# Low parts of weight blocks moved to GpSimd in a two-layer hybrid backbone

## The chip, the core and the metric

The kernel runs on one core of a Trainium2 chip. The metric is the device time of one execution in microseconds (us), as the median of several runs. The core has TensorE (matrix products, PE in the profile; its weight loads are PEld), VectorE (DVE), ScalarE (ACT), GpSimd (POOL) and the SyncE queue (SP), which here issues the DMAs.

## The reference, cut to what matters

Two layers work on 256 latent tokens and 256 context tokens of width 1024, in float32. Each layer does:

```python
h = rmsnorm(x, g1) * (1 + sc1) + sh1            # sc, sh, g: 6 modulation vectors from c @ w_mod
rx, rg, cq, ckv, kr, dq, dk, dv, mg = split(h @ w_in)
# 1. recurrence: conv of width 4 on rx, gates r, i = sigmoid(block-diagonal products),
#    a = exp(-8 r softplus(-lam)), b = sqrt(1 - a^2) i x,  h_t = a_t h_(t-1) + b_t, both ways
# 2. latent attention, 16 heads: o_b
# 3. differential attention, 8 heads of two maps:
o_c = (softmax(s q1 k1^T) - lam * softmax(s q2 k2^T)) @ v
# merge: three gated projections, then one output projection
x = x + g1 * ((ga * ((y_a * gelu(rg)) @ w_br_a) + gb * (o_b @ w_br_b) + gc * (norm(o_c) @ w_br_c)) @ w_out)
x = x + g2 * ffn(rmsnorm(x, g2) * (1 + sc2) + sh2)   # SwiGLU, hidden width 2816
```

The second layer computes queries and outputs for the 256 latent tokens only; its keys, values and recurrence still cover all 512.

## The kernel before

**Weights in two parts.** Every large product is made from three products of reduced-precision (`fp32r`) operands: a float32 matrix is split into a high part (the value rounded to `fp32r`) and a low part (the value less the high part), and `mm3` (lines 199 to 202) adds high x high, high x low and low x high in PSUM. In the trace these are the TensorE lines L200, L201 and L202.

Weights come in blocks of 128 x 1024 float32 (512 KB). `wload` (lines 156 to 181) takes a staging tile `st`, issues its DMA on SP's queue, takes a pair `wh`, `wl`, and calls `split`. In `split` (lines 136 to 141) ScalarE writes the high part with an activation, and VectorE writes the low part with one subtraction; both carry L138 in the trace, and the same line also splits activations, from PSUM or SBUF. Staging tiles and pairs come from rings of `WB = 3`. In layer 1 the ring is longer by two of each, which live in other tiles: pairs in `room`, staging tiles in a part of `acc`. So a low part shows as `wl<-st,wh` or as `room<-acc,room`.

**Order.** A planner (the tile framework) puts all instructions of each engine in one list by priority; each engine then works through its own list in order and waits at its head by semaphores. Weight splits get a priority ahead of their place in the program, by `first_by[0]` (90, or 600 in the recurrence of layer 1). Generators that yield pieces of matmul work stand in `queue`; `fill(ns)` lets them issue about that many ns of work between steps of the attentions and the recurrence.

**The two parts of a layer that the change touches.** First the differential attention. For four pairs of heads, `diff_proj` makes queries, keys and values (`gemm_tm`, six blocks a pair); meanwhile W_BB's projection of the latent attention's result (`gemm_fm`, eight blocks) runs. For each head `diff_prep` transposes and splits queries and keys, `diff_sc` makes the scores of both maps for each block of 128 queries, finds the row maximum (L621), exponentiates (L623) and merges the two maps (L966: `p1 = p2 * factor + p1`), `probs_T` transposes, `diff_pv` multiplies with the values. Then the recurrence, for four pairs of channel blocks: `rnn_rx` (projection and convolution, L1034), `rnn_rec` (gates from a block of `wlru`, L1056 to L1069, then two scans a block, L1082 and L1086), `rnn_rg` (projection and gelu, L1014 to L1017, product with the scan, L1108), with branch gates and W_BC's projections from `queue` (L1118, L1126, L1127). By the code these parts load 70 blocks in layer 0 and 72 in layer 1; the whole trace has 305 low parts on `wl` and 75 on `room`. In layer 0's recurrence the modulation vectors of later stages are made beside it (`mod_vectors`): VectorE multiplies streamed weights by the condition (L310), each such operation ordered behind the last low part by `issue_after(..., low[0])`, an edge without a semaphore.

**GpSimd before.** It holds only the Newton steps of some reciprocal roots (`rsqrt`, L222 to L225), for the queries of the latent attention (`rq`) and of the differential attention (`drq`), on tiles of 128 x 8 or 128 x 16.

Of the kernel before, what the change touches and what calls it, by code (L numbers as in the profile page):

```python
# [13 lines left out]
AF = mybir.ActivationFunctionType  # L14
ALU = mybir.AluOpType
# [48 lines left out]
def tile_hybrid(ctx: ExitStack, tc: tile.TileContext, xt, cvec, cwide, prm, row, dlam, rope, wmod, wmod0, wmodt, wfm, wcq, wckv, wuq, wukv, wlru, wfo, out):  # L64
    nc = tc.nc
    V = nc.vector
    A = nc.scalar
    G = nc.gpsimd
# [31 lines left out]
    def three_banks(stage):  # L100

        if spare[0] is not None:
            spare[0].close()
        spare[0] = ctx.enter_context(ExitStack())
        banks[0] = spare[0].enter_context(tc.tile_pool(name=stage, bufs=1, space=PSUM, reuse_waits="tile"))
# [27 lines left out]
    def f(ap):  # L133
        return ap.bitcast(F32)

    def split(dH, dL, src, scale=None):
        if scale is None:
            return A.activation(dH, src, AF.Copy), V.tensor_tensor(out=dL, in0=src, in1=f(dH), op=ALU.subtract)  # L138
        else:
            A.activation(dH, src, AF.Copy, scale=scale)  # L140
            V.scalar_tensor_tensor(out=dL, in0=src, scalar=scale, in1=f(dH), op0=ALU.mult, op1=ALU.subtract)

    ready = deque()
    hold = []
    low = [None]
    first_by = [WEIGHTS_FIRST]
    ring = {"st": 0, "w": 0}
    more = {"st": [], "w": []}

    def stage():  # L150
        ring["st"] = (ring["st"] + 1) % (WB + len(more["st"]))
        if ring["st"] < WB:
            return wp.tile([P, 1024], F32, tag="st", name="st")
        return more["st"][ring["st"] - WB]

    def wload(src, n=1024, now=True):

        if now and ready:
            key, H, L = ready.popleft()
            assert key == str(src)  # L160
            return H, L
        st = stage()
        nc.sync.dma_start(st[:, :n], src)
        ring["w"] = (ring["w"] + 1) % (WB + len(more["w"]))
        if ring["w"] < WB:
            H = wp.tile([P, 1024], F32R, tag="wh", name="wh")
            L = wp.tile([P, 1024], F32R, tag="wl", name="wl")
        else:
            H, L = more["w"][ring["w"] - WB]
        tc.cur_priority -= first_by[0]  # L170
        parts = split(H[:, :n], L[:, :n], st[:, :n])
        for b, a in zip(parts, hold):
            issue_after(b, a)
        hold.clear()
        low[0] = parts[1]
        tc.cur_priority += first_by[0]
        pace[1] += pace[0]
        while pace[1] >= 1:
            pace[1] -= 1
            slow_step(1)  # L180
        return H, L

    def ahead(srcs):

        ready.extend([(str(src), *wload(src, n, False)) for src, n in srcs])
# [5 lines left out]
    def slow_step(n):  # L191
        while n > 0 and slow:
            try:
                next(slow[0])
                n -= 1
            except StopIteration:
                slow.popleft()
# [30 lines left out]
    def issue_after(b, a):  # L228

        tc.add_manual_dep(b.ins, a.ins.name, mybir.DependencyInfo(mybir.DependencyClass.NoSync, mybir.DependencyReason.DATA), reason="one table for all")  # L230
# [6 lines left out]
    def fill(ns):  # L237

        credit[0] += ns
        while credit[0] > 0 and queue:  # L240
            try:
                credit[0] -= next(queue[0])
            except StopIteration:
                queue.popleft()
        if not queue:
            credit[0] = 0.0

    def flush():
        while queue:
            fill(1e6)  # L250
# [141 lines left out]
    def gemm_fm(l, widx, npair, xH, xL, TQ, ps_, consume, k_first=False):  # L392

        one = 2 * TQ <= 512
        for p in range(npair):
            if one:
                ps = ps_("ps0").rearrange("p (j n) -> p j n", j=2)
                pss = [ps[:, j, :] for j in range(2)]
            else:
                pss = [ps_(f"ps{j}")[:, :TQ] for j in range(2)]  # L400
            for hf in range(2):
                H, L = wload(*fm_block(l, widx, 2 * p + hf))
                H = H.rearrange("p (k n) -> p k n", n=256)
                L = L.rearrange("p (k n) -> p k n", n=256)
                order = [(j, kk) for kk in range(4) for j in range(2)] if k_first and p == 0 else [(j, kk) for j in range(2) for kk in range(4)]
                for i, (j, kk) in enumerate(order):
                    k = hf * 4 + kk
                    mm3(pss[j], H[:, kk, j * P:(j + 1) * P], L[:, kk, j * P:(j + 1) * P], xH[:, k, :TQ], xL[:, k, :TQ],
                        k == 0 and not (one and j == 1), k == KT - 1 and not (one and j == 0), one)
                    if k == KT - 1:  # L410
                        if not one:
                            consume(2 * p + j, 1, pss[j].unsqueeze(1))
                        elif j == 1:
                            consume(2 * p, 2, ps)
                    if i % 4 == 3 or k_first and p == 0 and i % 2 == 1:
                        yield (6 if k_first and p == 0 else 12) * mm_ns(TQ)

    def gemm_two(l, widx, xHL, consume):

        pss = [ps_any(f"ps{j}") for j in range(2)]  # L420
        for hf in range(2):
            H, L = wload(*fm_block(l, widx, hf))
            H = H.rearrange("p (k n) -> p k n", n=256)
            L = L.rearrange("p (k n) -> p k n", n=256)
            for j in range(2):
                for kk in range(4):
                    k = hf * 4 + kk
                    nc.tensor.matmul(pss[j], H[:, kk, j * P:(j + 1) * P], xHL(k), start=(k == 0), stop=False, skip_group_check=True)  # L428
                    nc.tensor.matmul(pss[j][:, :SEQ], L[:, kk, j * P:(j + 1) * P], xHL(k)[:, :SEQ], start=False, stop=(k == KT - 1), skip_group_check=True)  # L429
                if hf == 1:  # L430
                    consume(j, pss[j])
# [111 lines left out]
    for l in range(LAYERS):  # L543
# [7 lines left out]
        with ExitStack() as c1:  # L551
# [13 lines left out]
            def t_cq(name, dt=F32R):  # L565
                return tmp("cq", 10, dt=dt, name=name)
# [109 lines left out]
            def low_rank(wsrc, n, nf, toks, gcol, pss, extra, res, by_half=False):  # L676
# [26 lines left out]
                for i in range(nf):  # L703
                    pt = ps_tr("lrt")
                    for tt in toks:
                        nc.tensor.transpose(pt[:, tt * P:(tt + 1) * P], us[tt][:, i * P:(i + 1) * P], ident)
                    rH, rL = t_cq("rH"), t_cq("rL")
                    split(rH[:, :nt * P], rL[:, :nt * P], pt[:, :nt * P], scale=pm[:, gcol + i:gcol + i + 1])
                    res.append((rH, rL))
                    yield 4 * 109  # L710
# [70 lines left out]
            def mla_prep(h):  # L781
                qs, ks = mq[h // 4][0], mk[h // 2]
                ptq = ps_tr("trq")
                for tt in qtoks:
                    nc.tensor.transpose(ptq[:96, tt * P:(tt + 1) * P], qs[tt].rearrange("p (h d) -> p h d", d=96)[:, h % 4, :], ident)
                qH, qL = t_qk("qH"), t_qk("qL")
                split(qH[:96, :TQ], qL[:96, :TQ], ptq[:96, :TQ])
                ptk = ps_tr("trk")
                for tt in range(4):
                    nc.tensor.transpose(ptk[:96, tt * P:(tt + 1) * P], ks[tt][:, h % 2, :], ident)  # L790
                kH, kL = t_qk("kH"), t_qk("kL")
                split(kH[:96, :], kL[:96, :], ptk[:96, :], scale=gkk[:96])
                mqk[h] = (qH, qL, kH, kL)
# [328 lines left out]
            def branch_proj(widx, mgi, p, after=None):  # L1122
# [7 lines left out]

                yield from gemm_fm(l, widx + p, 1, oH, oL, TQ, ps_r[0], proj)

            three_banks(f"pair{l}")
            singles[0] = 1
            queue.append(diff_proj(0))
# [34 lines left out]
            for p in range(4):  # L1170
# [9 lines left out]
                for ns in rnn_rg(p):  # L1180
                    fill(ns * RG_SHARE[l])
            flush()
            for t in range(KT):
                y = t_cq("y", F32)
                nc.sync.dma_start(y[:, :TQ], yspill[:, t, :TQ])
                split(oH[:, t, :TQ], oL[:, t, :TQ], y[:, :TQ], scale=0.5)
# [309 lines left out]
```

## Time and profile before

| | |
|---|---|
| median of 3 runs | 1972.54 us (1972.23 to 1977.07) |
| the profiled execution's own time | 1974.12 us |
| its span, first to last instruction | 1972.3 us |
| busy: TensorE, VectorE, ScalarE, GpSimd | 1930.2, 1568.3, 1069.9, 58.8 us |
| TensorE's mean granted clock | 0.997 |

The profile is of one execution. Busy times are shares of its span; the ends of matmuls are modelled. "Idle before, releaser" is the time an engine stood idle just before a group of instructions, and what ended most of it.

### The profile page before, as it was taken

The page shows a single profiled execution, that of the slowest core. Times are in us where ns is not written, and L with a number is a line of the kernel's source. Part 1 is how long each engine was busy: PE and PEld are TensorE (multiplying, and loading weights), DVE is VectorE, ACT ScalarE, POOL GpSimd, SP SyncE. Part 2 cuts the span into 40 slices and gives each one's busy share as a digit, 9 for nine tenths or more (in the row PEclk, how much of TensorE's full clock was granted, in tenths as well). Part 3 has the DMA queues.
Part 4 walks back from the last instruction along what each step waited for, and adds up shares of the span by engine and source line. Part 5 has one row for each costly group of instructions (what it writes and reads, how often), then busy time and mean ns, then how long its engine had stood idle before and what let it go on. Part 6 is the DMA issues. An engine that isn't in the chain of part 4 may idle for free. (4 is left out here: it accounts for less than half of the span.)

```text
span 1972.3 us, 31832 instructions
## 1 busy us (share of the span) xinstructions
PE 1930.2 (98%) x11746; PEld 1666.3 (84%) x11746; DVE 1568.3 (80%) x3838; ACT 1069.9 (54%) x1975; POOL 58.8 (3%) x198
## 2 busy tenths in 40 slices
PE   7999999999999999999999999999999999899999
PEld 4888888988678878888888888988999788898888
DVE  5679965788798888789888876898688889966763
ACT  4568833455576663353233224798444678845552
POOL 0001000000000000000000000012010000000000
PEclk9999999999999999999999999999999999999999
DMA  8311122212234456536656653422322234474553
GB/s 291 99 41 51 53 65 77 76 55 67 70 102 129 140 191 197 184 127 201 196 191 201 200 176 115 151 64 76 128 93 80 65 123 143 156 231 150 185 189 108
DMA packets 91068, 258.16 MB, mean 131 GB/s; under 512 B 10144, under 2 KB 17312, under 8 KB 90656
## 3 DMA queue, kind: packets, MB, share of 16 engines
q1 hardware_dynamic: 90912, 256.13, 39.8%
q8 instruction: 92, 1.51, 0.3%
q14 instruction: 64, 0.52, 0.1%
HBM read 250.85 MB, written 5.24 MB: 130 GB/s over the span
## 5 line engine op out<-in xcount | busy, mean ns | idle before, releaser
L138 ACT ACTIVATE wh<-st 128x1024 fp32r<-128x1024 f32 (+4 forms) x305 | 308.4, 1012 | 367.8 <-PE ps L201 173.1
L138 DVE TENSOR_TENSOR wl<-st,wh 128x1024 fp32r<-128x1024 f32 (+4 forms) x305 | 354.2, 1162 | 125.5 <-ACT wh L138 122.0
L200 PE MATMUL ps<-hH,wh 128*128 128x512 f32 (+1 forms) x504 | 182.0, 361 | 3.8 <-ACT gt L1118 2.9
L202 PE MATMUL ps<-hH,wl 128*128 128x512 f32 (+1 forms) x504 | 180.6, 359 | 1.7 <-DVE wl L138 1.7
L201 PE MATMUL ps<-hL,wh 128*128 128x512 f32 (+1 forms) x504 | 181.3, 360 | 0.0
L200 PE MATMUL pst<-wh,hH 128*128 128x256 f32 x568 | 164.3, 289 | 0.0
L201 PE MATMUL pst<-wl,hH 128*128 128x256 f32 x568 | 162.1, 285 | 0.0
L202 PE MATMUL pst<-wh,hL 128*128 128x256 f32 x568 | 161.9, 285 | 0.0
L200 PE MATMUL ps<-h2H,wh 128*128 128x512 f32 (+1 forms) x368 | 139.1, 381 | 0.7 <-ACT h2H L379 0.7
L201 PE MATMUL ps<-h2L,wh 128*128 128x512 f32 (+1 forms) x368 | 139.5, 380 | 0.0
L202 PE MATMUL ps<-h2H,wl 128*128 128x512 f32 (+1 forms) x368 | 139.5, 380 | 0.0
L621 DVE TENSOR_REDUCE st<-S 128x1 f32<-128x512 f32 (+1 forms) x192 | 113.0, 596 | 21.4 <-ACT dp L623 11.2
L138 DVE TENSOR_TENSOR room<-acc,room 128x1024 fp32r<-128x1024 f32 (+3 forms) x75 | 87.6, 1169 | 30.6 <-ACT room L138 29.1
L200 PEld LDWEIGHTS pst<-wh,hH 128*128 128x128 f32 x568 | 108.6, 191 | 3.8 <-issue 3.3
L200 PEld LDWEIGHTS ps<-hH,wh 128*128 128x128 f32 x504 | 95.3, 189 | 19.3 <-ACT gt L1118 3.9
L202 PEld LDWEIGHTS pst<-wh,hL 128*128 128x128 f32 x568 | 108.5, 191 | 1.7 <-issue 1.4
L201 PEld LDWEIGHTS pst<-wl,hH 128*128 128x128 f32 x568 | 108.6, 191 | 1.1 <-issue 0.7
L202 PEld LDWEIGHTS ps<-hH,wl 128*128 128x128 f32 x504 | 95.2, 189 | 15.6 <-DVE wl L138 2.3
L310 DVE SCALAR_TENSOR_TENSOR ms<-ms,cb 128x512 f32<-128x512 f32 x160 | 107.3, 688 | 1.3
L138 ACT ACTIVATE room<-acc 128x1024 fp32r<-128x1024 f32 (+3 forms) x75 | 76.2, 1017 | 57.6 <-PE ps L201 20.5
L201 PEld LDWEIGHTS ps<-hL,wh 128*128 128x128 f32 x504 | 95.3, 189 | 12.8
L310 DVE SCALAR_TENSOR_TENSOR sq<-ms,cb 128x512 f32<-128x512 f32 x112 | 75.7, 689 | 31.9 <-DMA ms<-wmodt 31.0
(585 smaller groups left out, 5558.3 us busy)
## 6 DMA issues: line engine op xcount, KB each, us to landing
st<-wfm SPq DMA_DIRECT2D x224, 512.0 KB, 3.5
ms<-wmodt SPq DMA_DIRECT2D x160, 256.0 KB, 2.8
acc<-wfm SPq DMA_DIRECT2D x56, 512.0 KB, 3.5
st<-wfo SPq DMA_DIRECT2D x35, 512.0 KB, 3.5
mstage<-wmod SPq DMA_DIRECT2D x16, 512.0 KB, 5.3
acc<-wfo SPq DMA_DIRECT2D x9, 512.0 KB, 3.5
st<-wlru SPq DMA_DIRECT2D x7, 512.0 KB, 3.4
st<-wukv SPq DMA_DIRECT2D x13, 256.0 KB, 2.6
```

The lines of the kernel that those rows point to most:

```text
L138: return A.activation(dH, src, AF.Copy), V.tensor_tensor(out=dL, in0=src, in1=f(dH), op=ALU.subtract)
L200: nc.tensor.matmul(ps, wH, xH, start=start, stop=False, skip_group_check=skip)
L201: nc.tensor.matmul(ps, wH, xL, start=False, stop=False, skip_group_check=skip)
L202: nc.tensor.matmul(ps, wL, xH, start=False, stop=stop, skip_group_check=skip)
L310: issue_after(V.scalar_tensor_tensor(out=o, in0=st, scalar=1.0, in1=cb[:, v, :], op0=ALU.mult, op1=ALU.mult, accum_out=sums[:, i - i0, h, ...
L621: V.tensor_reduce(out=st[:, 0:1], in_=S, axis=AX.X, op=ALU.max, negate=True)
```

## The change

`split` gets an argument `by`, the engine that does the subtraction for the low part. `wload` passes `low_by[0]`, which is VectorE at first, GpSimd from the beginning of the differential attention of each layer to the end of its recurrence, and VectorE again after that. Splits of activations, which don't come through `wload`, stay on VectorE.

```diff
-    def split(dH, dL, src, scale=None):
+    def split(dH, dL, src, scale=None, by=V):
         if scale is None:
-            return A.activation(dH, src, AF.Copy), V.tensor_tensor(out=dL, in0=src, in1=f(dH), op=ALU.subtract)
+            return A.activation(dH, src, AF.Copy), by.tensor_tensor(out=dL, in0=src, in1=f(dH), op=ALU.subtract)
...
+    low_by = [V]
...
-        parts = split(H[:, :n], L[:, :n], st[:, :n])
+        parts = split(H[:, :n], L[:, :n], st[:, :n], by=low_by[0])
...
+            low_by[0] = G
             three_banks(f"pair{l}")
             singles[0] = 1
             queue.append(diff_proj(0))
...
             flush()
+            low_by[0] = V
             for t in range(KT):
                 y = t_cq("y", F32)
```

## Rows read from the trace of the kernel before

**Rows 1.** Summary of the page: busy time, share, instructions by engine.

```profile
PE 1930.2 (98%) x11746; PEld 1666.3 (84%) x11746; DVE 1568.3 (80%) x3838; ACT 1069.9 (54%) x1975; POOL 58.8 (3%) x198
```

**Rows 2.** Stretches: length, busy time of each engine, granted clock, DMA, GB/s.

```profile
262.00:545.00 283.00, 277.84 (x1885) 239.04 (x1880) 211.08 (x593) 136.04 (x311) 13.31 (x48) 1.00 0.22 71
545.00:727.00 182.00, 178.01 (x790) 144.50 (x789) 162.26 (x272) 132.30 (x198) 0.00 (x0) 1.00 0.43 137
1376.00:1590.00 214.00, 210.91 (x1603) 191.27 (x1602) 172.26 (x483) 106.73 (x221) 13.67 (x46) 1.00 0.28 89
1590.00:1720.00 130.00, 122.82 (x823) 112.89 (x822) 125.17 (x172) 110.14 (x153) 0.00 (x0) 0.99 0.43 140
```

**Rows 3.** TensorE's waits, 1590 to 1720: total us, times, longest us.

```profile
PE ps L202 <- DVE room L138: 5.5, 2, 4.1
```

**Rows 4.** VectorE's waits, 262 to 545.

```profile
DVE wl L138 <- ACT wh L138: 24.3, 14, 5.4
```

**Rows 5.** Groups of VectorE, 262 to 545: busy us, mean ns, idle before.

```profile
L138 DVE TENSOR_TENSOR wl<-st,wh 128x1024 fp32r<-128x1024 f32 x35 | 42.8, 1222 | 24.8 <-ACT wh L138 24.3
...
L966 DVE SCALAR_TENSOR_TENSOR dp<-dp,st,dp 128x512 f32<-128x512 f32 (+1 forms) x32 | 19.7, 615 | 0.7
```

**Rows 6.** Groups of VectorE by shape, 545 to 727.

```profile
L138 DVE TENSOR_TENSOR wl<-st,wh 128x1024 fp32r<-128x1024 f32 x33 | 40.2, 1218 | 7.9 <-ACT wh L138 7.8
...
L1017 DVE SCALAR_TENSOR_TENSOR ge<-ge,ps 128x512 f32<-128x512 f32 x8 | 5.5, 683 | 0.7 <-ACT ge L1016 0.7
L1126 DVE SCALAR_TENSOR_TENSOR gt<-gt,ps 128x512 f32<-128x512 f32 x8 | 5.4, 680 | 0.3 <-PE ps L202 0.2
...
L1015 DVE SCALAR_TENSOR_TENSOR ge<-ge,ps 128x512 f32<-128x512 f32 x8 | 5.4, 677 | 0.0
```

**Rows 7.** Groups of VectorE by shape, 1590 to 1720.

```profile
L138 DVE TENSOR_TENSOR wl<-st,wh 128x1024 fp32r<-128x1024 f32 x19 | 23.1, 1217 | 0.3 <-ACT wh L138 0.3
L138 DVE TENSOR_TENSOR room<-acc,room 128x1024 fp32r<-128x1024 f32 x13 | 15.9, 1220 | 0.8 <-ACT room L138 0.5 <-PE pg L201 0.3
...
L1126 DVE SCALAR_TENSOR_TENSOR gt<-gt,ps 128x512 f32<-128x512 f32 x4 | 2.7, 682 | 0.7 <-PE ps L202 0.7
L1015 DVE SCALAR_TENSOR_TENSOR ge<-ge,ps 128x512 f32<-128x512 f32 x4 | 2.7, 681 | 0.0
L1017 DVE SCALAR_TENSOR_TENSOR ge<-ge,ps 128x512 f32<-128x512 f32 x4 | 2.7, 676 | 0.0
```

**Rows 8.** GpSimd's lines in undisturbed stretches (264 to 269; 1420 to 1436.8): min/median/max ns.

```profile
L223 POOL TENSOR_TENSOR drqt<-drqt,drqv x3: 221/223/223, 265.2 to 267.6; 128x16 f32<-128x16 f32 x3
L223 POOL TENSOR_TENSOR drqt<-drqt,drqv x2: 202/202/202, 1435.2 to 1436.3; 128x8 f32<-128x8 f32 x2
L224 POOL TENSOR_SCALAR drqt<-drqt x3: 203/204/206, 265.5 to 267.9; 128x16 f32<-128x16 f32 x3
L224 POOL TENSOR_SCALAR drqt<-drqt x2: 197/198/198, 1435.5 to 1436.6; 128x8 f32<-128x8 f32 x2
```

**Rows 9.** Timeline of VectorE and GpSimd at three places: start us, length us.

```profile
459.06 1.22 DVE L138 TENSOR_TENSOR wl<-st,wh 128x1024 fp32r<-128x1024 f32 x1
459.26 1.09 POOL L223 TENSOR_TENSOR drqt<-drqt,drqv 128x16 f32<-128x16 f32 x1
...
1353.61 0.73 DVE L141 SCALAR_TENSOR_TENSOR kL<-trk,gkk,kH 96x512 fp32r<-96x512 f32 x1
1353.75 3.05 POOL L222 TENSOR_TENSOR rqt<-rq 128x8 f32<-128x8 f32 x1
1354.33 1.21 DVE L138 TENSOR_TENSOR wl<-st,wh 128x1024 fp32r<-128x1024 f32 x1
1355.54 1.21 DVE L138 TENSOR_TENSOR wl<-st,wh 128x1024 fp32r<-128x1024 f32 x1
...
221.07 0.68 DVE L138 TENSOR_TENSOR qL<-trq,qH 96x512 fp32r<-96x512 f32 x1
221.36 0.21 POOL L222 TENSOR_TENSOR rqt<-rq 128x16 f32<-128x16 f32 x1
```

## The prediction

> **What bounds the kernel now.** I read the summary first, then the stages, then the waits. TensorE's matmuls are busy in 1930.2 of 1972.3 us [rows 1], so whatever the edit takes off VectorE can at best give back TensorE's idle time. I cut the two parts of each layer that the edit touches by the first and last weight splits in the trace: 262 to 545 us (differential attention, layer 0), 545 to 727 (recurrence, layer 0), 1376 to 1590 and 1590 to 1720 (the same in layer 1). TensorE idles 283.0 - 277.8 = 5.2 us, 4.0 us, 3.1 us and 7.2 us in them [rows 2], 19.5 us together: the most that can be gained, at a granted clock of 1.00 or 0.99 throughout. The reader should then look at VectorE: 75% and 80% busy in the attentions, 89% in layer 0's recurrence, but 125.2 of 130 us in layer 1's. That last stage is VectorE's own. The waits say so too: TensorE's longest waits there are for a low part, 5.5 us in two waits, one of 4.1 us [rows 3], because `room` (the second home of weight blocks in layer 1) stood behind other VectorE work. In the attention of layer 0, the opposite: VectorE, which takes its instructions in order, stood idle 24.3 us at the head of its queue waiting for ScalarE's high part [rows 4]. Nothing behind it could run.
>
> **What the change removes.** By the code 70 blocks of layer 0 and 72 of layer 1 pass `wload` between the two settings of `low_by[0]`. The trace has 35 low parts in the first stretch (42.8 us) [rows 5], 33 in the second (40.2 us) [rows 6], and 19 + 13 in the fourth (23.1 + 15.9 = 39.0 us) [rows 7]; the others lie over the edges of the stretches or in the attention of layer 1. They leave VectorE at 1.22 us each: 142 x 1.22 = 173 us of its work, and with them the idle time at its head.
>
> **What it adds on GpSimd.** The same subtraction, 128x1024, two inputs in SBUF. No GpSimd instruction of that size is in the trace, so I bound it. Undisturbed, the two-input operation takes 202 ns for 8 columns and 222 for 16, which is 2.5 ns a column; the one-input one 198 and 204 ns, 0.75 ns a column [rows 8]. For 1024 columns: 0.20 + 1016 x 0.00075 = 0.96 us below, 0.20 + 1016 x 0.0025 = 2.7 us above. I take 2.7 us, since the new instruction is of the two-input kind, and count 2.5 us of it as streaming. ScalarE's part, the DMAs and their number stay.
>
> The Trainium skill (GPSIMD Engine Reference, section Performance versus the Vector engine) gives 4497 ns for such an operation over 2048 columns, about twice VectorE's; by that page I estimate 2.25 us for 1024. No run shows it yet; with it the sum for layer 1's recurrence below would be 78 + 32 x 2.05 = 144 us instead of 158, and the forecast 14 us lower.
>
> **What the two engines do to each other.** This decides the sign. The trace shows it in one direction. A tiny GpSimd operation that starts inside a low part on VectorE does not end until that low part does: 0.20 us of work takes 1.09 us and ends at 460.35, the low part at 460.28; another takes 3.05 us, through one scaled split and two low parts in a row, losing the race at each change of instruction [rows 9]. Beside a VectorE operation that reads PSUM and one SBUF tensor it takes its normal 0.21 us [rows 9]. So VectorE instructions with two SBUF operands shut GpSimd out for their whole length, and one that has PSUM, an SBUF scalar and an SBUF tensor (the 0.73 us row) seems to do it too. How long a GpSimd instruction shuts out VectorE no row shows, as all are too short. Bounds: nothing, and its whole streaming time. I take the whole, the mirror of the row.
>
> The Trainium skill (SBUF — State Buffer, section SBUF: two separate sides) says the same for both directions: whoever starts first holds the shared pair for the whole instruction. The trace agrees for VectorE's 1.22 us; for GpSimd's side no run shows it yet.
>
> **Layer 1's recurrence.** VectorE is busy 125.2 us; without its low parts (39.0) 86.2; of these three groups read PSUM and one SBUF tensor (`gt` 2.7, `ge` 2.7 and 2.7) [rows 7]. That leaves 125.2 - 39.0 - 8.1 = 78.1 us that exclude GpSimd. To these come 32 x 2.5 = 80.0 us of GpSimd. Sum 158 us in a stretch that took 130: +28. If GpSimd's price is the lower bound, 78.1 + 32 x 0.8 = 104 us, the stage falls back on TensorE's 122.8: -7. I take +20: by the two-input price, less 8 us in which VectorE's PSUM readers run beside GpSimd.
>
> **Layer 0's recurrence.** 162.3 - 40.2 - 16.4 (three PSUM groups) [rows 2, 6] = 105.7 us, and 33 x 2.5 = 82.5 us: 188 in 182, +6; below, TensorE's 4.0 us of idle comes back. I take +2; some of the 105.7 are small operations, which hold nothing for long.
>
> **The attentions.** GpSimd would be busy 35 x 2.7 = 95 of 283 us, a third of the time. VectorE saves 42.8 us and up to 24.3 us of idle, but each merge of the two softmax maps (L966, SBUF operands, 32 there [rows 5] and by the code 16 in layer 1) meets a running low part one time in three and waits half of 2.7 us: 48 x 0.33 x 1.35 = 21 us in both layers, on the path from scores to transposes. TensorE hides both, since projections from the queue fill its time (98% and 99% busy). I take 0, between -8 (5.2 + 3.1 us of idle come back) and +10 (half of the 21 uncovered, where the queue runs dry late in the stage).
>
> **Queues.** GpSimd has so far had only the reciprocal roots of the queries (L222 to L225, twelve operations of 0.2 us). They now stand behind low parts that wait for ScalarE. Their user is the first softmax of a head pair, after the pair's key projection, 48 matmuls of 256 columns, so I cost this at nothing; without that cover it is one low part, 2.7 us, for each of 8 head pairs. The staging buffer `st` is free for SP's next load only when its low part is done, 1.5 us later than now; three buffers (five in layer 1) cover that, and so does the read-ahead for `wl` itself, except where GpSimd starves (below). The modulation sums (L310) were ordered behind the low part on the same engine; across engines that edge orders only the planner's list.
>
> **Sum.** 20 + 2 + 0 = +22 on the profiled execution's 1974.1 us: 1996. The median of the runs shown is 1972.5, 1.6 us under it, so 1995 for the median.
>
> **The rivals.** *Faster.* GpSimd doesn't hold VectorE up for long, or is quick; then VectorE is relieved of 39 us where it was the bound, the 4.1 us wait on `room` goes, and TensorE's idle comes back. For it: [rows 3, 4]; against it: the exclusion in [rows 9]. Half of 19.5 us is -10: 1963, all of it 1953. The point that decides: in layer 1's recurrence (130 - 78) / 32 = 1.6 us per low part. Chance 0.22, 1953 to 1967.
>
> *A wash.* The lock costs layer 1's recurrence what the attentions and layer 0 give back: 1967 to 1978. Chance 0.13.
>
> *Starved GpSimd.* VectorE issues two-operand instructions back to back, and a low part loses the race as in the 3.05 us row: 2.85 us of wait and 2.7 of work make 5.55 us a block, while layer 1's recurrence uses one each 130 / 32 = 4.06 us. 32 x 1.49 = 48 us; layer 0 uses one each 182 / 33 = 5.5 us and is spared. 1974.1 + 48 - 1.6 = 2020. For it: that row; against it: VectorE itself runs dry when TensorE waits, which lets GpSimd in. Chance 0.13, 2010 to 2040. That the subtraction stays on VectorE cannot be: GpSimd takes this operation already [rows 8].
>
> **How the numbers follow.** The forecast (both engines share by exclusion, GpSimd's price above the 1.6 us that decides) has 0.52, and gives 1980 to 2010. A measurement of this kernel can tell about 0.3%, 6 us, from no change. Slower by more: 0.52 + 0.13 = 0.65; within: 0.13; faster: 0.22. The range 1960 to 2022 leaves out about half of the fastest case and two thirds of the slowest, 0.1 each; the forecast's own range is 1980 to 2010.
>
> **What would show it.** Right: GpSimd's busy time rises by 142 x 2.5 us or more, to about 400 us, with low parts from 2.5 us to over 4 us; VectorE's SBUF operations in the recurrences (L1067, scans) get longer than now by up to 2.5 us each; layer 1's recurrence lasts about 150 us and TensorE waits in it for `wl` and `room` on GpSimd; layer 0's recurrence within 6 us of 182; attentions within 5 us. Wrong: low parts at 1.6 us or less, VectorE's durations unchanged, and layer 1's recurrence near 123 us. A different order of TensorE's work, from the planner's view of a free VectorE, could move stages in ways that no row shows.

## The result and the profile after

The changed kernel takes 2119.72 us (median of 4 runs, 2115.57 to 2120.91) against 1973.98 us for the kernel before (4 runs): ratio 1.0732 [1.0718, 1.0747], 145.7 us slower. The direction was forecast, the size was not: the prediction said 1995, its range ended at 2022, and no rival reached beyond 2040. The profiled execution took 2119.68 us; its span of 2117.6 us is 145.3 us over that of before. In the new file the lines stand one lower from L146 on (L622 is now L623, L1086 is L1087), and one more after each of the two lines added further down.

The summary of the page, to be held against [rows 1]:

```profile
span 2117.6 us, 31850 instructions
PE 1977.5 (93%) x11746; PEld 1698.4 (80%) x11746; DVE 1631.1 (77%) x3696; ACT 1075.7 (51%) x1975; POOL 406.3 (19%) x340
```

VectorE executes 142 instructions fewer and is busy 62.8 us longer. The low parts taken off it were 142 x 1.22 = 173 us. TensorE runs the same 11,746 matmuls, yet is busy 47.3 us longer; its idle time rises from 1972.3 - 1930.2 = 42.1 to 2117.6 - 1977.5 = 140.1 us. 47.3 + 98.0 = 145.3, the whole span's difference.

Where the time was lost, in us, by the start of the first and last row of each stage in TensorE's and VectorE's timelines of the two traces (first key transposes `dtrk`, last transposes of the attention's output `subt`, last scan `hh`; equal instructions in a row share one):

| stage | lasted before | lasts after | adds | forecast |
|---|---|---|---|---|
| up to layer 0's attention | 296.4 | 299.8 | +3.4 | 0 |
| differential attention, layer 0 | 268.1 | 296.3 | +28.2 | 0 |
| recurrence, layer 0 | 152.9 | 185.5 | +32.6 | +2 |
| up to layer 1's differential attention | 679.4 | 695.0 | +15.6 | 0 |
| differential attention, layer 1 | 190.6 | 222.3 | +31.7 | 0 |
| recurrence, layer 1 | 126.4 | 159.7 | +33.3 | +20 |
| the rest | 258.5 | 259.0 | +0.5 | 0 |

The 15.6 us belong to the edit too: low parts of blocks loaded ahead are on GpSimd from 1399 us, some 80 us before the first key transposes. The same four parts by stretches (columns as in [rows 2]; they are cut at these marks, rounded, and so hold not quite the same matmuls as the stretches there):

```profile
300.00:596.00 296.00, 263.56 (x1746) 225.52 (x1744) 216.84 (x560) 140.87 (x324) 85.95 (x68) 0.97 0.20 64
596.00:790.00 194.00, 176.85 (x723) 141.17 (x724) 165.26 (x205) 121.54 (x173) 75.39 (x28) 0.94 0.36 118
1480.00:1700.00 220.00, 196.14 (x1378) 173.80 (x1378) 156.27 (x408) 94.48 (x201) 76.86 (x65) 0.93 0.21 68
1700.00:1866.00 166.00, 136.70 (x867) 124.38 (x866) 151.34 (x147) 113.11 (x155) 82.55 (x31) 0.90 0.35 118
```

TensorE now idles 32.4, 17.2, 23.9 and 29.3 us in them, against 5.2, 4.0, 3.1 and 7.2 in [rows 2], and the granted clock is 0.97 down to 0.90 where it was 1.00 or 0.99. GpSimd is nowhere near full: 29% to 50%. GpSimd's low parts by line (min/median/max ns, first and last start):

```profile
L138 POOL TENSOR_TENSOR wl<-st,wh x114: 2345/2407/3448, 216.4 to 1834.6; 128x1024 fp32r<-128x1024 f32 x114
L138 POOL TENSOR_TENSOR room<-acc,room x28: 2340/2406/2862, 1410.3 to 1839.1; 128x1024 fp32r<-128x1024 f32 x28
```

TensorE's longest waits over the span (total us, times, longest), where [rows 3] had `room` alone:

```profile
PE pg L201 <- ACT tz L1057: 25.1, 8, 9.6
PE dtrk L940 <- DVE ddk L923: 15.6, 8, 4.0
PE S L664 <- ACT dp L624: 14.9, 11, 3.8
...
PE ps L203 <- POOL wl L138: 7.9, 5, 2.0
...
PE ps L203 <- DVE room L138: 5.1, 1, 5.1
```

TensorE rarely waits for a low part that GpSimd makes late: 7.9 us here and 1.5 for `room`. It waits most for gates, for keys to transpose and for the softmax, which are the chains that go through VectorE. What holds them is seen at one place of layer 1's recurrence, in the timeline of VectorE, GpSimd, ScalarE and TensorE (start, length, us):

```profile
1735.30 6.72 POOL L138 TENSOR_TENSOR wl<-st,wh 128x1024 fp32r<-128x1024 f32 x2 [3.64 <-ACT wh L138]
1736.45 3.37 DVE L1087 TENSOR_TENSOR_SCAN hh<-a,tz 128x512 f32<-128x512 f32 x1
1739.74 2.83 DVE L1082 TENSOR_TENSOR fb<-tz,g 128x512 f32<-128x512 f32 x1
1741.97 5.40 POOL L138 TENSOR_TENSOR room<-acc,room 128x1024 fp32r<-128x1024 f32 x2
1742.50 2.62 DVE L1089 TENSOR_TENSOR hh<-hh 128x256 f32<-128x256 f32 x1
1745.04 3.41 DVE L1083 TENSOR_TENSOR_SCAN hh<-a,fb 128x512 f32<-128x512 f32 x1
1747.39 0.39 PE L203 MATMUL pg<-xH,wl 128*128 128x512 f32 x1
1748.38 0.66 DVE L1086 TENSOR_TENSOR tz<-tz,xc 128x512 f32<-128x512 f32 x1
1749.07 1.22 DVE L1087 TENSOR_TENSOR_SCAN hh<-a,tz 128x512 f32<-128x512 f32 x1
1750.79 0.42 DVE L1089 TENSOR_TENSOR hh<-hh 128x256 f32<-128x256 f32 x1
...
1755.14 0.63 ACT L138 ACTIVATE xH<-xc 128x512 fp32r<-128x512 f32 x1 [10.71 <-DVE xc L1035]
1756.47 2.31 DVE L1035 SCALAR_TENSOR_TENSOR xc<-ps,prm,xc 128x508 f32<-128x508 f32 x3
1757.46 2.38 POOL L138 TENSOR_TENSOR wl<-st,wh 128x1024 fp32r<-128x1024 f32 x1 [10.09 <-ACT wh L138]
...
1758.02 0.80 PE L201 MATMUL pg<-xH,wh 128*128 128x512 f32 x1 [9.56 <-ACT tz L1057]
```

The two engines take turns: four low parts in a row, and four VectorE instructions that each last one low part longer than they need. The same scan, product and sum take 1.22, 0.66 and 0.42 us a moment later, when GpSimd is idle. That is 3.37 + 2.83 + 2.62 + 3.41 - 1.22 - 0.66 - 0.42 - 1.22 = 8.7 us. Behind them in VectorE's list stands the convolution of the next pair (L1035); ScalarE waits 10.7 us for it, and TensorE 9.6 us for the gates. Note too the last low part: it starts in the midst of three L1035, which read PSUM, an SBUF scalar and an SBUF tensor, and neither side is held.

The clock around this wait (length, TensorE busy and count, ..., granted clock, DMA, GB/s):

```profile
1740.00:1748.00 8.00, 8.00 (x51) 7.21 (x50) 8.00 (x3) 2.28 (x3) 7.37 (x3) 1.00 0.36 123
1748.00:1752.00 4.00, 0.45 (x3) 0.03 (x1) 3.96 (x8) 0.00 (x0) 0.00 (x0) 0.98 0.00 0
1752.00:1756.00 4.00, 0.00 (x0) 0.00 (x0) 3.24 (x6) 0.86 (x2) 0.00 (x0) 0.50 0.74 246
1756.00:1760.00 4.00, 1.99 (x6) 1.71 (x7) 3.93 (x5) 3.97 (x7) 2.38 (x1) 0.50 0.20 82
1760.00:1764.00 4.00, 4.00 (x22) 3.72 (x22) 3.40 (x6) 3.52 (x6) 0.00 (x0) 0.74 0.36 131
```

With TensorE idle the granted clock falls from 1.00 to 0.50 (from 2.4 to 1.2 GHz), and it is still low when the work comes back: the first gate matmul takes 0.80 us, where those before the wait took 0.39. So a wait is paid twice. Over the whole trace TensorE is busy 94.2 us at a granted clock of 0.50, against 9.4 us before. Half of the difference, some 42 us by this estimate, is what the lower clock adds, which is most of the 47.3 us by which the same matmuls are busy longer.

In the attention the held instructions are tiny. Timeline at a softmax of layer 0:

```profile
408.56 0.74 DVE L967 SCALAR_TENSOR_TENSOR dp<-dp,st,dp 128x512 f32<-128x512 f32 x1
408.88 2.68 POOL L138 TENSOR_TENSOR wl<-st,wh 128x1024 fp32r<-128x1024 f32 x1 [6.04 <-ACT wh L138]
409.22 2.35 DVE L623 TENSOR_TENSOR st<-st,drq 128x1 f32<-128x1 f32 x1
...
411.69 0.56 ACT L624 ACTIVATE dp<-S,st,drq 128x256 f32<-128x256 f32 x1 [2.88 <-DVE st L623]
...
414.26 0.39 PE L664 MATMUL S<-dkH,dqH 64*128 64x256 f32 x2 [2.02 <-ACT dp L624]
...
414.82 0.39 PE L202 MATMUL pst<-wl,hH 128*128 128x256 f32 x1
```

A product of one column, 0.155 us in the mean before, lasts 2.35 us and ends with the low part, at 411.57. The exponential waits 2.9 us for it, the next one follows late, the scores that wait for these exponentials stand 2.0 us on TensorE, and the projection that could have filled the gap (414.82) stands behind the scores in TensorE's list.

The groups of VectorE by shape over the whole span show how general that is (busy us, mean ns, idle before):

```profile
L623 DVE TENSOR_TENSOR st<-st,drq 128x1 f32<-128x1 f32 x96 | 29.0, 302 | 2.1 <-DVE st L622 0.5
L966 DVE SCALAR_TENSOR_TENSOR st<-st,s,nlam 128x1 f32<-128x1 f32 x48 | 25.0, 520 | 1.3
L1068 DVE SCALAR_TENSOR_TENSOR tz<-scr,tz 128x512 f32<-128x512 f32 x32 | 33.1, 1033 | 9.5 <-ACT scr L1067 6.6 <-ACT tz L1062 2.1
L1087 DVE TENSOR_TENSOR_SCAN hh<-a,tz 128x512 f32<-128x512 f32 x16 | 27.5, 1720 | 0.1
...
L138 DVE TENSOR_TENSOR pL<-ptr,pH 128x512 fp32r<-128x512 f32 x40 | 27.1, 688 | 12.9 <-ACT pH L138 12.5
```

Before, their means were 155, 219, 688, 1211 and 686 ns; two of the groups in the trace of before:

```profile
L622 DVE TENSOR_TENSOR st<-st,drq 128x1 f32<-128x1 f32 x96 | 14.9, 155 | 1.1
...
L1086 DVE TENSOR_TENSOR_SCAN hh<-a,tz 128x512 f32<-128x512 f32 x16 | 19.4, 1211 | 0.0
```

The last of the five reads PSUM and is not held. Count times (mean after less mean before), summed over all groups of one shape, gives the time that VectorE was held: 209.5 us, of which 74.4 in instructions of 16 columns or fewer, 32.2 from 32 to 256, and 102.9 from 512 up. The largest share of one line, 31.6 us, falls on the modulation sums (L311) beside layer 0's recurrence. Per low part that is 209.5 / 142 = 1.48 us held and 145.7 / 142 = 1.03 us of kernel time.

### The profile page after: what moved, and what is told of

Same layout as the page of the kernel before. It is cut to its first block, busy times and chain, and to the rows that moved or that the text cites. A ratio compares the mean times of both kernels' runs of the same rounds, so it can differ in the third digit from the quotient of the medians.

```text
span 2117.6 us, 31850 instructions
## 1 busy us (share of the span) xinstructions
PE 1977.5 (93%) x11746; PEld 1698.4 (80%) x11746; DVE 1631.1 (77%) x3696; ACT 1075.7 (51%) x1975; POOL 406.3 (19%) x340
## 4 chain that ended last, share of the span: by engine, by line
PE 49%; DVE 14%; issue 3%; DMA 3%; ACT 2%; POOL 0%; SPq 0%; ACTq 0%; DVEq 0%; POOLq 0%
PE ps L203 8%; PE ps L201 8%; PE ps L202 8%; PE ps L429 4%; PE po L203 2%; PE po L201 2%; PE po L202 2%; PE ps L430 2%; DMA ms<-wmodt 2%; PE ptr L636 1%; PE pst L201 1%; PE pst L202 1%; PE pst L203 1%; PE po L1368 1%; DVE tz L1068 1%
## 5 line engine op out<-in xcount | busy, mean ns | idle before, releaser
L138 POOL TENSOR_TENSOR wl<-st,wh 128x1024 fp32r<-128x1024 f32 x114 | 290.6, 2554 | 534.3 <-ACT wh L138 517.9
L138 DVE TENSOR_TENSOR wl<-st,wh 128x1024 fp32r<-128x1024 f32 (+4 forms) x191 | 215.1, 1128 | 87.5 <-ACT wh L138 84.9
L223 POOL TENSOR_TENSOR rqt<-rq 128x16 f32<-128x16 f32 (+1 forms) x24 | 7.1, 295 | 778.7 <-DVE rq L215 739.9
L622 DVE TENSOR_REDUCE st<-S 128x1 f32<-128x512 f32 (+1 forms) x192 | 113.1, 597 | 33.7 <-ACT dp L624 15.5
L311 DVE SCALAR_TENSOR_TENSOR ms<-ms,cb 128x512 f32<-128x512 f32 x160 | 117.1, 749 | 1.4
```

The lines of the kernel that those rows point to most:

```text
L138: return A.activation(dH, src, AF.Copy), by.tensor_tensor(out=dL, in0=src, in1=f(dH), op=ALU.subtract)
L223: G.tensor_tensor(out=t, in0=y, in1=y, op=ALU.mult)
L311: issue_after(V.scalar_tensor_tensor(out=o, in0=st, scalar=1.0, in1=cb[:, v, :], op0=ALU.mult, op1=ALU.mult, accum_out=sums[:, i - i0, h, ...
L622: V.tensor_reduce(out=st[:, 0:1], in_=S, axis=AX.X, op=ALU.max, negate=True)
```

## The experiments

The runs below came in three batches, each beside the kernel before on the same chip (medians 1974.38, 1973.35, 1974.5); "held" is worked out as above.

| run | median us | ratio | against before | held us |
|---|---|---|---|---|
| the change | 2119.72 | 1.0732 [1.0718, 1.0747] | +145.7 | 209.5 |
| attention_only | 2047.11 | 1.037 [1.034, 1.04] | +72.7 | 83.9 |
| recurrence_only | 2053.74 | 1.0403 [1.0373, 1.0433] | +79.4 | 125.9 |
| echo_on_gpsimd | 2106.11 | 1.0669 [1.0638, 1.0699] | +131.7 | 160.8 |
| fill_on_gpsimd | 1993.46 | 1.0098 [1.0069, 1.0127] | +19.1 | 40.5 |
| four_slices | 2054.9 | 1.0408 [1.0376, 1.0441] | +81.6 | 132.8 |
| half_echo | 2035.39 | 1.031 [1.0279, 1.034] | +62.0 | 82.6 |
| attention_small_ops | 2031.17 | 1.0288 [1.0258, 1.0318] | +57.8 | 70.8 |
| before_small_ops | 1978.23 | 1.0021 [1.0009, 1.0032] | +4.9 | 1.7 |
| fill_once | 1962.53 | 0.9936 [0.992, 0.9953] | -12.0 | 8.3 |
| echo_copy | 2010.54 | 1.0184 [1.0168, 1.0199] | +36.0 | 55.5 |
| echo_fill | 1990.02 | 1.0081 [1.0066, 1.0096] | +15.5 | 19.9 |
| ffn_only | 1977.76 | 1.0017 [1.0008, 1.0026] | +3.3 | 33.3 |

**attention_only and recurrence_only** do one part of the change alone.

```diff
                 fill(DIFF_STEP[l])
             flush()
+            low_by[0] = V
             three_banks(f"single{l}")
```
```diff
-            low_by[0] = G
             three_banks(f"pair{l}")
...
+            low_by[0] = G
             three_banks(f"single{l}")
```

> Low parts on GpSimd in the differential attention of both layers only, on VectorE in the recurrence. My prediction had the attentions at nothing; the trace after shows their two stretches some 29 us longer each and layer 1's stretch before it 15 to 19 us longer. If the sum of the stages is what counts: +70 to +95 us over before (2045 to 2070). If the attentions are only late because of what the recurrence does to the order of the work: within 15 us of before.

> Low parts on GpSimd in the recurrence of both layers only. If the stages add up: +55 to +75 us (2030 to 2050), 30 to 35 us a layer. By my prediction's own terms (20 + 2 us): about 1996.

+72.7 and +79.4 (4 us above the range expected): together 152, about the 146 of the whole. Each part costs by itself. That the attention alone costs 73 us ends the forecast's 0 for it.

**echo_on_gpsimd** leaves the low part on VectorE, and lets GpSimd do a subtraction of the same size afterwards whose result nobody reads.

```diff
-        parts = split(H[:, :n], L[:, :n], st[:, :n], by=low_by[0])
+        parts = split(H[:, :n], L[:, :n], st[:, :n])
+        if low_by[0] is G:
+            G.tensor_tensor(out=st[:, :n], in0=f(H[:, :n]), in1=f(H[:, :n]), op=ALU.subtract)
```

> Low parts stay on VectorE, in an order nearly that of before. After each, in the attention and the recurrence, GpSimd does one more subtraction of the same size whose result nobody uses (high part less high part, written over the staging tile). No low part is late. If what costs the time is that the two engines exclude one another: +60 to +150 us, although nothing waits for GpSimd's result but the staging tile's next load. If it is the late low parts or the planner's other order: within 10 us of before.

+131.7 us, 90% of the change's cost, though nothing waits for what GpSimd writes but the next load of its staging tile. TensorE's list of 11,746 matmuls differs from before's in 11 places (the change's in 1882). So neither a wait for GpSimd's low parts nor another order of the work is needed for such a cost: it is enough that GpSimd subtracts beside VectorE. What a later release of the staging tile adds is bounded by echo_fill below, +15.5 us with GpSimd at work for longer. How the other 14 us of the change arise isn't separated: its subtraction is longer (2.41 against 1.90 us, medians), its low parts come later, and its VectorE has less to do. The echo's group of GpSimd by shape, and a group of VectorE in the same run (688 ns before):

```profile
L174 POOL TENSOR_TENSOR st<-wh 128x1024 f32<-128x1024 f32 x114 | 238.3, 2092 | 551.5 <-DVE wl L138 346.1 <-DVE st L628 44.1 <-ACT dp L626 25.5
...
L1070 DVE SCALAR_TENSOR_TENSOR tz<-scr,tz 128x512 f32<-128x512 f32 x32 | 35.2, 1102 | 0.8 <-ACT scr L1069 0.5
```

**half_echo** does that after every second block only (the diff is against the echo).

```diff
+    odd = [0]
...
+        odd[0] += 1
-        if low_by[0] is G:
+        if low_by[0] is G and odd[0] % 2:
             G.tensor_tensor(out=st[:, :n], in0=f(H[:, :n]), in1=f(H[:, :n]), op=ALU.subtract)
```

> As the echo experiment (low parts on VectorE, the order of before, an unused subtraction on GpSimd), but after every second block only. If every GpSimd subtraction costs its own stalls on a path that has no room: half of the echo's 132 us, 2030 to 2050. If the cost comes only where the two engines' work no longer fits into a stretch (my prediction's sum for the recurrence): less than a third, under 2018.

+62.0 us for 71 instructions, +131.7 for 142: 0.87 and 0.93 us each, with TensorE's list identical to before's. The cost goes by the instruction. Down to half of the load there is no point below which GpSimd's work fits in beside VectorE's, which is how the prediction had worked out the recurrences.

**fill_on_gpsimd** and **fill_once** replace the subtraction by writes: a copy of one column, then three fills (or one). They leave the low part of these blocks out of the products.

```diff
-            return A.activation(dH, src, AF.Copy), by.tensor_tensor(out=dL, in0=src, in1=f(dH), op=ALU.subtract)
+            high = A.activation(dH, src, AF.Copy)
+            if by is G:
+                G.tensor_copy(out=dL[:, 0:1], in_=f(dH)[:, 0:1])
+                for _ in range(3):
+                    last_ = G.memset(f(dL), 0.0)
+                return high, last_
...
```

> The changed kernel, but GpSimd makes the low parts by three fills with zero and a copy of one column, in place of the subtraction: the low parts are left out of the products. The order of the work is nearly that of the changed kernel and a low part is about as late (three fills, an estimate of 2 to 3 us from 0.20 us for 128 columns), but GpSimd hardly reads SBUF. If the exclusion of operations that read SBUF is the cause: 1955 to 1995. If lateness or order is: 2090 to 2125. If a fill excludes VectorE as well: in between or as slow as the changed kernel.

> As the fill experiment (low parts left out of the products, nearly the changed kernel's order), with one fill of about 0.96 us in place of three, so that the low part is as early as it was on VectorE. If the 19 us that the three fills cost come from lateness: 1965 to 1980. If they come from the planner's other order of the work: 1985 to 1997. Below 1965 there would be time to win by relieving VectorE.

Three fills keep GpSimd busy longer than the change does (493.2 us against 406.3) and deliver the block later, and cost 19.1 us instead of 145.7. With one fill the kernel is 12.0 us faster than before, below both ranges expected, with a list of TensorE that differs from the changed kernel's in 122 of 11,746 places: so the other order of the work costs nothing, and 12 us is about what relieving VectorE of 173 us of low parts can be worth here when next to nothing holds it. The 31 us between the two fills are not separated further. With three fills TensorE waits 7.3 us for GpSimd's blocks, where with one these waits are nearly gone, and VectorE is held for 40.5 us instead of 8.3. Groups by shape of fill_on_gpsimd; the second had a mean of 174 ns before, the third 155:

```profile
L142 POOL MEMSET wl<- 128x1024 f32 x342 | 325.9, 955 | 18.1
...
L220 DVE TENSOR_SCALAR drk<-drkv 128x16 int32<-128x16 int32 x8 | 7.8, 978 | 0.3
...
L629 DVE TENSOR_TENSOR st<-st,drq 128x1 f32<-128x1 f32 x96 | 14.9, 156 | 1.8
```

A GpSimd instruction that only writes doesn't hold VectorE's two-input operations (scans 1212 ns, against 1211 before). What is held here is nearly all of one kind, TENSOR_SCALAR (34 of the 40.5 us), up to about the length of a fill.

**echo_copy** and **echo_fill** are the echo with a one-input copy, and with fills (against the echo).

```diff
-            G.tensor_tensor(out=st[:, :n], in0=f(H[:, :n]), in1=f(H[:, :n]), op=ALU.subtract)
+            G.tensor_copy(out=st[:, :n], in_=f(H[:, :n]))
```
```diff
-            G.tensor_tensor(out=st[:, :n], in0=f(H[:, :n]), in1=f(H[:, :n]), op=ALU.subtract)
+            G.tensor_copy(out=st[:, 0:1], in_=f(H[:, 0:1]))
+            for _ in range(3):
+                G.memset(st[:, :n], 0.0)
```

> As the echo experiment, with a copy (one input) of 1024 columns on GpSimd in place of the subtraction. If any operation of GpSimd that reads SBUF excludes VectorE, the cost goes with its duration: a copy of 1.0 to 1.2 us against 2.4 gives 2000 to 2050. If only operations with two inputs do: within 10 us of before.

> As the echo experiment, with a copy of one column and three fills of 1024 columns over the staging tile, 2.9 us on GpSimd and hardly a read. If writes exclude VectorE as reads do: 2060 to 2140. If only reads do: within 12 us of before, the rest from a later release of the staging tiles.

The copy holds VectorE as well, so one input on GpSimd's side is enough; it takes 0.59 of the subtraction's time and costs 0.27 as much, so the price grows faster than the length. Its group:

```profile
L174 POOL COPY st<-wh 128x1024 f32<-128x1024 f32 x114 | 140.3, 1232 | 573.3 <-DVE wl L138 443.8 <-issue 28.7 <-ACT dp L626 27.1
```

The fills cost 15.5 us, which lies between the two cases expected: 17.8 of their 19.9 us of held time lie in instructions of 16 columns or fewer, the TENSOR_SCALARs again.

**four_slices** makes GpSimd's low part in four instructions of 256 columns.

```diff
...
+            c = src.shape[1] // 4 if by is G else src.shape[1]
+            if by is G:
+                for i in range(4):
+                    last_ = G.tensor_tensor(out=dL[:, i * c:(i + 1) * c], in0=src[:, i * c:(i + 1) * c], in1=f(dH[:, i * c:(i + 1) * c]), op=ALU.subtract)
+                return high, last_
...
```

> The changed kernel with each subtraction on GpSimd cut into four of 256 columns, in nearly the same order. The work on GpSimd is the same, plus three fixed parts of about 0.2 us a block. If the exclusion lasts one whole GpSimd instruction and the cost is what short VectorE operations wait behind it: waits shrink from up to 2.4 us to up to 0.8, and the time falls to 2010 to 2060. If the cost is the sum of the time in which the shared access is taken (my prediction's sum): no faster than the changed kernel's 2120, since that sum grows.

GpSimd is busy longer, 531.3 us (four times 0.89 us a block, waits for VectorE among them), and the kernel is 65 us faster than with whole low parts: what counts more is how long one instruction holds, not how long GpSimd works. The groups by shape, the scan at 1518 ns where whole low parts make it 1720:

```profile
L142 POOL TENSOR_TENSOR wl<-st,wh 128x256 fp32r<-128x256 f32 x456 | 393.0, 895 | 398.4 <-ACT wh L138 379.9 <-PE pg L209 10.8 <-DMA y<-yspill 7.7
...
L1093 DVE TENSOR_TENSOR_SCAN hh<-a,tz 128x512 f32<-128x512 f32 x16 | 24.3, 1518 | 0.1
```

**attention_small_ops** is attention_only with the two one-column operations of each softmax on ScalarE; **before_small_ops** is its control, the same edit on the kernel before.

```diff
...
-                V.tensor_tensor(out=st[:, 1:2], in0=st[:, 0:1], in1=sc_ap, op=ALU.mult)
+                A.activation(st[:, 1:2], st[:, 0:1], AF.Copy, scale=sc_ap)
...
-                    V.scalar_tensor_tensor(out=rr[1], in0=rr[1], scalar=s0[:, tt:tt + 1], in1=nlam, op0=ALU.mult, op1=ALU.mult)
+                    A.activation(rr[1], rr[1], AF.Copy, scale=s0[:, tt:tt + 1])
+                    A.activation(rr[1], rr[1], AF.Copy, scale=nlam)
```

> As the run with low parts on GpSimd in the attention only, and the two operations of 128x1 between a row maximum and the merge of the softmax maps (scale times maximum; factor of the second map) on ScalarE instead of VectorE, so that they can't be held. If these tiny operations carry most of the attention's cost of 73 us: 1990 to 2015, to be read against the next run. If the merges and other operations over 256 or 512 columns carry it: 2035 to 2050.

> Control: the kernel before with the same two operations of 128x1 on ScalarE. Each goes from 0.16 and 0.22 us on VectorE to one and two ScalarE operations, on the path from scores to probabilities. Expected within 15 us of before, 1965 to 1990.

The attention's price falls from 72.7 to 2031.17 - 1978.23 = 52.9 us, between the two ranges expected. So about 20 of the 73 us, not most of them, come from 144 instructions of one column, which the prediction had not counted at all. Other small ones are left: 37.8 of the 70.8 us of held time still lie in 16 columns or fewer.

**ffn_only** sets `low_by[0]` to GpSimd in the first loop of layer 1's feed-forward part alone.

```diff
-            low_by[0] = G
             three_banks(f"pair{l}")
...
+            low_by[0] = G if last else V
             for p in range(FT // 2):
...
+            low_by[0] = V
```

> Low parts on GpSimd only in the FFN's input projections of layer 1 (44 blocks), nearly the order of before. There 44 x 2.4 = 106 us of GpSimd meet only some 20 us of VectorE operations with SBUF operands, and a block is used each 3.0 us. If a low part costs the same everywhere (146 us for 142): +35 to +50 us. If it costs what VectorE's two-operand work on TensorE's path makes of it: -3 to +12 us.

GpSimd makes 40 low parts and holds VectorE 33.3 us, 25 us of it in twenty instructions (1.7 and 0.85 us each), and the kernel is only 3.3 us slower. The two groups were at 693 and 692 ns before:

```profile
L138 POOL TENSOR_TENSOR wl<-st,wh 128x1024 fp32r<-128x1024 f32 x24 | 64.4, 2701 | 265.7 <-ACT wh L138 265.7
...
L1318 DVE SCALAR_TENSOR_TENSOR th<-th,sum 128x512 f32<-128x512 f32 x10 | 23.7, 2368 | 7.0 <-ACT th L1317 7.0
...
L1323 DVE TENSOR_TENSOR th<-th,sum 128x512 f32<-128x512 f32 x10 | 15.4, 1538 | 0.3
```

So held time is no price by itself. It becomes one where TensorE's next instruction waits on the chain that runs through VectorE, as in softmax and recurrence.

## Why the prediction was right in kind and wrong in size

**The step that failed first: "TensorE hides both, since projections from the queue fill its time (98% and 99% busy). I take 0".** Measured: +28.2 and +31.7 us, and 19 us around them. Two things were wrong in it. The instructions met were too few: only 48 merges were counted, for 21 us, but each operation with two SBUF operands is held, whatever its size. Of the 39.9 us by which VectorE was held in layer 0's attention, 33.5 lie in instructions of 16 columns or fewer. And the cover failed: 98% busy told that TensorE had other work, not that it could get at it. Its list is fixed, and it stops at the scores of 414.26 with the filler right behind them. That is read at this one place; no run moved the filler ahead.

**The step that failed second: the recurrences as a sum that has to fit the stretch** (188 us in 182: "I take +2"; 158 in 130: "I take +20"). Measured +32.6 and +33.3. Exclusion doesn't wait until the sum is over the length: half_echo shows a price for each instruction, since a VectorE operation held now delays what stands behind it now, and later idle time doesn't give that back. The unreduced +28 (158 in 130) was near the measured +33.3 by luck, as the sum had two slips and left out that TensorE's clock would fall. Its 78.1 us hold 11.9 us of L1034, which reads PSUM and excludes nothing (below), and the 8 us that make +28 into +20 were PSUM readers that the 78.1 had left out already. Put right, its terms give 66 + 80 = 146 in 130, +16: near the forecast's +20, so it is the model that failed and not the sum.

**The clock** was no term of the sum. [rows 2] gave 1.00 in the stretches, and the waits took it to 0.90 to 0.97 there, some 42 of the 47.3 us of longer TensorE time.

**Exclusion itself was right, in both directions.** The forecast took "the whole, the mirror of the row"; the echo, the scan of 3.41 us and the one-column product of 2.35 us show it. One reading of [rows 9] was not right: that PSUM with an SBUF scalar and an SBUF tensor "seems to" exclude. Of the VectorE instructions of the changed kernel that began inside a low part (0.05 us or more behind its start, 0.25 us or more before its end), none of the 62 that read PSUM was lengthened, nine of them with an SBUF scalar and an SBUF tensor, while all 100 with two SBUF tensors and all 12 TENSOR_SCALARs were. In the other direction eight of the eleven small GpSimd operations that began inside such a scaled split before, with 0.25 us or more of it left, took their normal 0.20 to 0.22 us. What kept the one of [rows 9] from ending within its split stays open.

The Trainium skill (SBUF — State Buffer, section SBUF: two separate sides) says that the shared pair is held for a whole instruction by whoever starts first, and that two SBUF inputs on VectorE matter only against a GpSimd operation that reads SBUF. The traces agree: 302 ns mean for the one-column product beside subtractions, 156 beside fills, 155 alone. That fills still hold TENSOR_SCALARs (174 to 978 ns) fits its other case, VectorE operations in a two-port mode, if these are such, which no row here states.

**GpSimd's price**: 2.7 us forecast, 2.41 measured as the median. Right to 12%, and by itself it would have made the forecast lower. The Trainium skill (GPSIMD Engine Reference, section Performance versus the Vector engine) had led to an estimate of 2.25, which is nearer.

**The rivals.** *Faster* gave 1963: fill_once, the case in which next to nothing is held (8.3 us), takes 1962.5, so the gain at stake was sized about rightly and the exclusion took it away. *Starved GpSimd* is wrong: no low part lasts over 3.45 us, and TensorE waits 9.4 us for GpSimd's low parts in all. A *wash* it was not. The warning of the planner's other order was empty: the echo keeps before's order and costs 90% of the change, and fill_once nearly keeps the changed order and costs nothing. The reciprocal roots behind low parts, taken at nothing, were rightly so: the trace shows no wait of TensorE or VectorE for one.

**What was to show it**: GpSimd's busy time of about 400 us (406.3) and longer L1068 and scans came. Layer 1's recurrence got longer, but by 33 us instead of 20, and TensorE waited there only 1.5 us for GpSimd. Low parts ran from 2.34 to 3.45 us, not from 2.5 to over 4. Attentions within 5 us and layer 0's recurrence within 6 did not come.

**Left open**: what the waits would cost without the lower clock that they bring (the 42 us are an estimate from one trace, and no run kept the clock up); how much of the cost falls on held operations off TensorE's path, such as the modulation sums; and why four slices, at a mean under 0.9 us, still cost 81.6 us.

## What to carry to other kernels

Work that reads SBUF, moved to GpSimd beside VectorE operations with two SBUF operands, is paid by what VectorE is held, one instruction at a time and the one-column ones too, wherever TensorE's next instruction hangs on that chain; a busy share of 98% is no cover where the filler stands behind the waiting instruction. Price such a move first with an echo: let the other engine do the operation in the old order, with its result unused. If it must be GpSimd, short instructions, ones that only write, or a stage whose VectorE chain has slack (the feed-forward part here: 40 low parts for 3.3 us) cost least.

## What the runs showed of the hardware that was not expected

- VectorE and GpSimd can fall into turns, each instruction letting in one of the other: four scans and products took 2.62 to 3.41 us instead of 0.42 to 1.22.
- A one-input GpSimd copy of 1024 columns (1.23 us) holds VectorE too; a fill (0.955 us) holds hardly anything but TENSOR_SCALARs, one group of them from a mean of 0.174 to 0.978 us.
- VectorE's reductions, reciprocals and all operations that read PSUM ran at their normal length inside GpSimd's low parts (none of 82 lengthened).
- After a wait of 9.6 us TensorE's granted clock was 0.50, and its next matmul of 512 columns took 0.80 us instead of 0.39.
